# The second FFN of a two-layer backbone: up projection by Strassen's seven products, inner rows kept in DRAM, down projection by resident weight groups

## The chip, the cores and the metric

One core of a Trainium2 chip runs the whole program. The metric is the device time of one execution in microseconds (us), the median of the runs taken. Engines are called by their names in the profile: PE (TensorE matmul), PEld (TensorE weight load), DVE (VectorE), ACT (ScalarE), POOL (GpSimd), SP (SyncE, which here only issues DMAs).

## The reference, cut to what matters

Two layers work on 1152 tokens (1024 latent and 128 context tokens) of width 1024. Each layer has a mixer and then a gated ConvFFN, both between a norm before and a norm and residual after. The change is in the FFN of layer 1, the last work of the program:

```
def conv_ffn(h, w_up, cw, cb, w_down):      # h [1152, 1024], w_up [1024, 5632], w_down [2816, 1024]
    u = dwconv(h @ w_up, cw, 1) + cb        # three taps along the tokens, latent and context apart
    g, val = jnp.split(u, 2, axis=-1)       # 2816 gate and 2816 value channels
    return (jax.nn.gelu(g) * val) @ w_down
```

Everything is float32. The kernel reaches this on PE by splitting each factor x into a high part that the fp32r format holds and a rest, x = xh + xl, and by adding three products: xh yh, xh yl and xl yh (`mm3`, line 80).

## The kernel before, in words

The tokens lie in nine tiles of 128. The inner 2816 channels lie in 22 blocks of 128. The output projection of the mixer (`mixer_out`, L1311) takes the token tiles one after the other: 48 matmuls of 512 columns into two PSUM banks, then `post` (sum of squares on ACT, root on POOL, scaling and residual on DVE) and `pre` (L272: the norm before the FFN, eight transposes on PE, scale and shift on ACT into `h`, the high part on DVE into `hh`, the rest on POOL into `hl`). `hh` and `hl` are whole arrays [128, 8, 1152]: eight slices of the width, all tokens.

`ffn` (L1352) then goes over the 22 blocks. For each it loads the gate's and the value's columns of the up weights (two loads of 512 KB, `wcol`), splits them (ACT the high part `whi`, DVE the rest `wlo`), and for each of three chunks of tokens (386, 386 and 384 columns) and each of the two halves makes 24 matmuls (8 slices of the width, 3 products each; `pps`). The convolution is read straight from PSUM (ACT the middle tap and the bias, DVE the two others into `cc`), then gelu on ACT, the product on DVE, and the split into `mh` (ACT) and `ml` (DVE). After each second block `down` (L1405) adds two blocks' share of the down projection to the sums `acc` of all nine tiles: per tile and half 6 matmuls of 512 columns (`dps`), and a DVE addition. `ffn_end` (L1422) makes the last norm and residual and stores the result.

Buffers come from pools: a tag with n buffers hands them out in turn, and a buffer is filled again when its last reader is done. A pool that is opened over the room of closed ones can be used when those are released. The order of the instructions on each engine is fixed when the program is built, by a planner that takes the program's order as the priority and its own estimate of durations; each engine then works through its queue in that order and waits where an input isn't there.

## Time and profile before

| | |
|---|---|
| runs | 3004.41, 3001.33, 2997.97 us; median 3001.33 |
| profiled execution | span 2997.2 us (the page gives no device time of this execution of its own; the span lies within the runs shown) |
| busy | PE 94%, PEld 85%, DVE 68%, ACT 37%, POOL 27% of the span |
| layer 1's output projection ends, second FFN begins | about 2158 us into the span |
| last matmul begins | 2988.4 us into the span |

PE's busy time is modelled: a matmul of 384 columns is shown as 0.33 us long although the next one starts 0.17 us later. What a matmul costs in a stream is therefore read from the distance between starts.

### The profile page before, as it was taken

The numbers are of one execution on the slowest core, as the hardware profiler recorded it, in microseconds if no ns is written. First come the engines' busy times: TensorE is split into PE (matmuls) and PEld (weight loads), VectorE is DVE, ScalarE is ACT, GpSimd is POOL, SyncE is SP. The second block draws the span as 40 slices with busy tenths as digits, with TensorE's granted clock in tenths as the row PEclk, the third lists the DMA queues.
The fourth block names the chain that finished last, engine by engine and source line by source line (L and its number), as shares of the span: only waits on it lengthen the run. The fifth ranks groups of instructions, "written<-read, shape, count | busy, mean of one in ns | idle before, by whom it ended". The sixth has DMA issues, their size and how long they took to land.

```text
span 2997.2 us, 40584 instructions
## 1 busy us (share of the span) xinstructions
PE 2816.8 (94%) x15196; PEld 2557.3 (85%) x15196; DVE 2035.9 (68%) x3572; ACT 1096.7 (37%) x1921; POOL 813.7 (27%) x982
## 2 busy tenths in 40 slices
PE   7976788888999999999999989999999999999998
PEld 3874566777789999999999979997899999999997
DVE  6777765988668888888655685455455555555557
ACT  5222113766454222322222365554532222222222
POOL 2699972877131000000000151112300000000001
PEclk9998899999999999999999999999999999999999
DMA  6434447552642333323211131124411111111113
GB/s 222 142 86 107 117 138 200 137 116 75 193 146 89 98 99 96 97 91 93 62 43 57 64 122 55 53 88 146 138 46 43 43 43 43 43 43 43 43 36 134
DMA packets 298835, 279.45 MB, mean 93 GB/s; under 512 B 45454, under 2 KB 259682, under 8 KB 298638
## 3 DMA queue, kind: packets, MB, share of 16 engines
q1 hardware_dynamic: 266168, 238.51, 25.8%
q0 software_dynamic: 14912, 23.21, 3.1%
q10 hardware_dynamic: 17558, 15.14, 1.8%
q8 instruction: 119, 1.95, 0.3%
q14 instruction: 78, 0.64, 0.1%
HBM read 220.59 MB, written 56.20 MB: 92 GB/s over the span
## 4 chain that ended last, share of the span: by engine, by line
PE 69%; DVE 6%; ACT 3%; issue 2%; DMA 1%; POOL 1%; ACTq 0%; DVEq 0%; POOLq 0%; SPq 0%
PE pps L87 43%; PE dps L87 16%; PE ops L87 6%; DVE e L1077 1%; DVE nb L1060 1%; PE sA L1055 1%; ACT e L1066 1%; PE gps L87 1%; PE tps L284 1%; DVE wh L1102 0%; DVE s L1114 0%; PE ops L1145 0%; DMA mw<-w_mod 0%; POOL hl L290 0%; PE gps L759 0%
## 5 line engine op out<-in xcount | busy, mean ns | idle before, releaser
L87 PE MATMUL pps<-hh,whi 128*128 128x384 f32 (+1 forms) x2880 | 977.0, 339 | 1.1 <-ACT whi L97 0.7
L87 PE MATMUL pps<-hh,wlo 128*128 128x384 f32 (+1 forms) x2880 | 974.7, 339 | 2.2 <-DVE wlo L99 2.2
L87 PE MATMUL pps<-hl,whi 128*128 128x384 f32 (+1 forms) x2880 | 974.7, 339 | 0.6 <-POOL hl L798 0.4
L87 PEld LDWEIGHTS pps<-hh,whi 128*128 128x128 f32 x2880 | 546.1, 190 | 17.5 <-issue 3.2
L87 PEld LDWEIGHTS pps<-hh,wlo 128*128 128x128 f32 x2880 | 545.6, 189 | 15.2 <-DVE wlo L99 3.2
L87 PEld LDWEIGHTS pps<-hl,whi 128*128 128x128 f32 x2880 | 546.4, 190 | 8.1 <-DVE hl L798 0.7
L99 POOL TENSOR_TENSOR wlo<-wr,whi 128x1024 fp32r<-128x1024 f32 x44 | 109.2, 2487 | 1455.3 <-PE dps L87 1162.5
L1374 DVE SCALAR_TENSOR_TENSOR cc<-pps,cvc,cc 128x255 f32<-128x255 f32 (+1 forms) x704 | 342.0, 511 | 145.0 <-ACT cc L1371 139.8
L1420 DVE TENSOR_TENSOR acc<-acc,dps 128x512 f32<-128x512 f32 x360 | 245.9, 683 | 232.5 <-PE dps L87 231.5
L1371 ACT ACTIVATE cc<-pps,cvc 128x383 f32<-128x383 f32 (+2 forms) x264 | 175.0, 665 | 414.1 <-PE pps L87 393.3
L87 PE MATMUL dps<-whi,mh 128*128 128x512 f32 x792 | 311.8, 394 | 1.2 <-DVE acc L1420 1.2
L87 PE MATMUL dps<-whi,ml 128*128 128x512 f32 x792 | 312.0, 394 | 0.0
L87 PE MATMUL dps<-wlo,mh 128*128 128x512 f32 x792 | 310.5, 392 | 0.0
L97 ACT ACTIVATE whi<-wr 128x1024 fp32r<-128x1024 f32 x168 | 177.7, 1059 | 278.3 <-PE pps L87 196.6
L99 DVE TENSOR_TENSOR wlo<-wr,whi 128x1024 fp32r<-128x1024 f32 x124 | 153.9, 1243 | 85.4 <-PE pps L87 70.4
L231 DVE SCALAR_TENSOR_TENSOR macc<-mw,sil,macc 128x256 f32<-128x256 f32 x392 | 174.9, 482 | 18.9 <-DMA mw<-w_mod 18.1
L87 PEld LDWEIGHTS dps<-whi,ml 128*128 128x128 f32 x792 | 148.8, 188 | 33.7
L87 PEld LDWEIGHTS dps<-whi,mh 128*128 128x128 f32 x792 | 149.2, 188 | 20.8 <-DVE acc L1420 2.4
L87 PEld LDWEIGHTS dps<-wlo,mh 128*128 128x128 f32 x792 | 149.2, 188 | 18.8
L1389 ACT ACTIVATE cc<-cc 128x385 f32<-128x385 f32 x132 | 69.3, 525 | 248.1 <-DVE cc L1374 232.2
L1104 POOL TENSOR_TENSOR wl<-wf,wh 128x512 fp32r<-128x512 f32 (+2 forms) x96 | 144.4, 1523 | 52.5 <-DVE ra L1074 44.1
L1394 DVE TENSOR_TENSOR ml<-cc,mh 128x385 fp32r<-128x385 f32 x132 | 118.2, 899 | 34.2 <-ACT mh L1393 34.2
(356 smaller groups left out, 4171.6 us busy)
## 6 DMA issues: line engine op xcount, KB each, us to landing
wr<-ffn_w_up SPq DMA_DIRECT2D x88, 512.0 KB
mw<-w_mod SPq DMA_DIRECT2D x224, 128.0 KB
x<-x SPq DMA_DIRECT2D x45, 512.0 KB
wr<-ffn_w_down SPq DMA_DIRECT2D x44, 512.0 KB
wm<-w_mod SPq DMA_DIRECT2D x40, 512.0 KB
k<-kh POOLq DMA_DIRECT2D x8, 1408.0 KB, 6.4
wr<-w_in_cd SPq DMA_DIRECT2D x20, 512.0 KB
yr<-y SPq DMA_DIRECT2D x17, 512.0 KB
```

What stands on the lines that cost most here:

```text
L87: nc.tensor.matmul(ps, x, y, start=first and i == 0 and j == 0, stop=last and i == n - 1 and j == 2)
L97: nc.scalar.activation(hi, raw, AF.Copy)
L99: (eng or nc.vector).tensor_tensor(lo, raw, f(hi), op=OP.subtract)
L231: nc.vector.scalar_tensor_tensor(acc[v], wt, s, acc[v], op0=OP.mult, op1=OP.add)
L284: nc.tensor.transpose(ps[:, i], tmp[:, b * 128:(b + 1) * 128], self.id)
L1055: pin(nc.tensor.matmul(A[:, c:c + w], heads[u.h, 2][:, m, u.q0:u.q0 + 128], heads[u.h, m][:, j, u.k0 + c:u.k0 + c + w], start=j == 0, stop ...
L1104: pin((nc.vector if late else nc.gpsimd).tensor_tensor(vl, u.wf[b][:, :k], f(vh), op=OP.subtract))
L1371: nc.scalar.activation(cc[:, :no], ps[:, q:q + no], AF.Identity, bias=cw[3], scale=cw[1])
L1374: nc.vector.scalar_tensor_tensor(cc[:, oa - o0:ob - o0], ps[:, oa + d - i0:ob + d - i0], cw[j], cc[:, oa - o0:ob - o0], op0=OP.mult, op1=O ...
L1389: nc.scalar.activation(cc[:, :no], cc[:, :no], AF.Gelu_apprx_tanh)
L1394: nc.vector.tensor_tensor(ml[:, o0:o1], g[1][:, :no], f(mh[:, o0:o1]), op=OP.subtract)
L1420: nc.vector.tensor_tensor(acc[t][:, sl], acc[t][:, sl], ps, op=OP.add)
```

## The change

Only layer 1's FFN is changed; layer 0's still runs `ffn` and `ffn_end`. Beside that, the pools are opened in another order, one small load of layer 0's output projection (`rb`) takes a buffer of `cv` and no longer one of its own pool, and comments are gone.

The up projection of one block, gate and value together, is a product of a 2 x 2 arrangement of weights (gate or value by first or second half of the width) with a 2 x 2 arrangement of inputs (half of the width by half of the tokens, 576 each). The new code makes it by seven products instead of eight (Strassen's in Winograd's form). Each has 4 slices of the width, 3 split products and two matmuls of 288 columns, 24 matmuls into two PSUM banks (`prod`). Sums of weights are formed on POOL in the weight tiles themselves and then split (`pair`); sums of inputs (`forms`: T1, T2, T3, T4, each in a high part and a rest) are formed once. The results are put together by additions on DVE (with one addend in PSUM) and POOL. `up_rest` then runs the convolution from SBUF over whole rows of 1152 tokens, and writes the high part and the rest of the inner rows to DRAM. `down2` keeps the split down weights of 8, 7 and 7 blocks in SBUF and for each group goes over the nine tiles, with the inner rows read back through POOL's DMA queue; the sums start in the first group (ACT), grow in the others (DVE), and in the third the tile's norm, residual and store follow at once (`ffn_fin`).

All these buffers lie in pools that are opened after the pools of the stage before are closed: `big` (inputs by quarters) on the right side, `big2` (T2, T1, T4), `wru` (raw weights and split pairs, 8 buffers) and `midu` (8 buffers) on the left over the room of the output projection, and four PSUM buffers of two banks each, which are all eight banks. The down stage's pools in turn lie over those of the up stage.

```
+    def pair(self, raw, eng, pool=None):
+        p = (pool or self.wr).tile([128, 2] + shape[1:], F32R, ...)
+        self.nc.scalar.activation(p[:, 0], raw, AF.Copy)
+        eng.tensor_tensor(p[:, 1], raw, f(p[:, 0]), op=OP.subtract)
+    def prod(self, p, y):
+        ps = self.bank2("sps")
+        w = HT // 2
+        steps = [(p[:, x, k], y[j][:, k]) for k in range(4) for x, j in ((0, 0), (0, 1), (1, 0))]
+        for n, (x, y) in enumerate(steps):
+            for c in range(2):
+                nc.tensor.matmul(ps[:, c, :w], x, y[:, c * w:c * w + w], start=n == 0, stop=n == len(steps) - 1)
+    def forms(self, H):
...
+        for k in range(4):
+            A, B, C = (self.mid_tile([128, 2, HT], "tf") for _ in range(3))
+            whole(C[:, 0], 0, 1, k, V)
+            whole(A[:, 0], 0, 0, k, G)
+            whole(A[:, 1], 1, 1, k, V)
+            V.tensor_tensor(A[:, 0], C[:, 0], A[:, 0], op=OP.subtract)
+            V.tensor_tensor(B[:, 0], A[:, 1], A[:, 0], op=OP.subtract)
+            put(T2, k, B[:, 0], V)
+            put(T1, k, A[:, 0], V)
+            whole(B[:, 1], 1, 0, k, G)
+            V.tensor_tensor(A[:, 1], A[:, 1], C[:, 0], op=OP.subtract)
+            put(T3, k, A[:, 1], G)
+            V.tensor_tensor(B[:, 1], B[:, 0], B[:, 1], op=OP.subtract)
+            put(T4, k, B[:, 1], G)
+        def block(fb):                       # in up()
...
+            tt(G, S1, A21, A22, OP.add)
+            tt(G, S2, S1, A11, OP.subtract)
...
+            A.activation(x, P(A11, B11, V), AF.Copy)
+            tt(G, A21, A11, A21, OP.subtract)
+            p = P(A12, B21, G)
+            tt(V, c11, x, p, OP.add)
+            tt(G, A12, A12, S2, OP.subtract)
+            A.activation(q_, P(A12, B22, V), AF.Copy)
+            yield
+            T1, T2, T3, T4 = F
+            p = P(S2, T2, G)
+            tt(V, x, x, p, OP.add)
...
+            A.activation(y, P(S1, T1, V), AF.Copy)
+            tt(G, c12, x, y, OP.add)
+            tt(G, c12, c12, q_, OP.add)
+            p = P(A21, T3, G)
+            tt(V, z, x, p, OP.add)
...
+            p = P(A22, T4, V)
+            tt(G, c22, z, y, OP.add)
+            tt(V, c21, z, p, OP.subtract)
+            self.up_rest(l, fb, C)
+            yield
+        next(bs[0])
+        next(bs[1])
+        F.extend(self.forms(H))
+        for fb in range(NFB):
+            next(bs[fb])
+            if fb > 0 and fb + 1 < NFB:
+                next(bs[fb + 1])
+    def up_rest(self, l, fb, C):             # for s in 0 (gate), 1 (value): ACT middle tap, four DVE taps from SBUF, gelu
...
+        nc.vector.tensor_tensor(m, h, m, op=OP.mult)
+        nc.scalar.activation(h.bitcast(F32R), m, AF.Copy)
+        nc.vector.tensor_tensor(m, m, h, op=OP.subtract)
+        for x, y in enumerate((h, m)):
+            nc.sync.dma_start(self.scratch(f"m{l}", [2, NFB, 128, T])[x, fb], y)
+    def down2(self, l, finish):              # GROUPS = (range(0, 8), range(8, 15), range(15, 22))
...
+        for gi, fbs in enumerate(self.GROUPS):
+            for t in range(NT):
+                mt = self.dm.tile([128, 2, n, 128], F32R, tag="dm", name=self.nm("mt"))
+                for x in range(2):
+                    nc.gpsimd.dma_start(mt[:, x], m[x, fbs[0]:fbs[-1] + 1, :, t * 128:t * 128 + 128].rearrange("f p t -> p f t"))
...
+                            nc.tensor.matmul(ps[:, h], mt[:, x, i], W[fb][:, y, h * 512:h * 512 + 512], ...)
+                if gi == 0:
+                    nc.scalar.activation(acc[t], pv, AF.Copy)
+                else:
+                    nc.vector.tensor_tensor(acc[t], acc[t], pv, op=OP.add)
...
+        self.big2, self.wr, self.mid = P("big2", 6), P("wru", 8), P("midu", 8)
+        self.ps = P("psu", 4, space=PSUM)
+        self.up(1, H)
```

## Rows read from the trace of the kernel before

**Rows 1.** The page: busy us and share of each engine, instructions
```profile
PE 2816.8 (94%) x15196; PEld 2557.3 (85%) x15196; DVE 2035.9 (68%) x3572; ACT 1096.7 (37%) x1921; POOL 813.7 (27%) x982
```

**Rows 2.** Windows (stretch; busy per engine; clock; DMA share; GB/s): the second FFN
```profile
2170.70:2988.90 818.20, 818.07 (x4296) 767.12 (x4293) 467.07 (x739) 226.96 (x350) 62.59 (x40) 1.00 0.16 50
```

**Rows 3.** The chain of waits, in order of time: one period of the FFN
```profile
2311.03 2.76 PE dps L87 x12
...
2386.43 2.76 PE dps L87 x12
```

**Rows 4.** PE's timeline (start, us, operation): distance of starts at 384 and 512 columns
```profile
2201.86 0.34 PE L87 MATMUL pps<-hh,whi 128*128 128x384 f32 x1
...
2210.02 0.33 PE L87 MATMUL pps<-hh,wlo 128*128 128x384 f32 x1
...
2984.07 0.39 PE L87 MATMUL dps<-wlo,mh 128*128 128x512 f32 x1
...
2988.38 0.39 PE L87 MATMUL dps<-whi,ml 128*128 128x512 f32 x1
```

**Rows 5.** PE's timeline in the S5 gate: a stream of 24 at 288 columns
```profile
744.21 3.31 PE L759 MATMUL gps<-gg,gw 128*128 128x288 f32 x24
747.36 0.50 PE L1109 MATMUL ops<-ones,o 128*128 128x1 f32 x4
```

**Rows 6.** Timeline where the output projection ends and the FFN begins
```profile
2157.89 1.03 PE L284 MATMUL tps<-misc,tmp 128*128 128x128 f32 x8
2159.98 1.28 DVE L270 SCALAR_TENSOR_TENSOR x<-tmp,rs,x 128x1024 f32<-128x1024 f32 x1 [0.35 <-POOL rs L144]
2167.41 0.75 DVE L277 TENSOR_SCALAR tmp<-x,q 128x1024 f32<-128x1024 f32 x1 [2.10 <-POOL q L144]
2170.58 2.91 ACT L287 ACTIVATE h<-tps,mc,mc 128x128 f32<-128x128 f32 x8 [1.86 <-PE tps L284]
```

**Rows 7.** Timeline where attention's PSUM pools replace those of the projections
```profile
498.25 0.49 ACT L940 ACTIVATE qr<-pps 128x384 f32<-128x384 f32 x1 [3.67 <-PE pps L87]
498.84 2.56 PE L1055 MATMUL sA<-k,q 128*128 128x512 f32 x12 [0.63 <-issue]
```

**Rows 8.** Timelines of POOL and DVE: the same operations alone and side by side
```profile
2172.63 1.29 POOL L290 TENSOR_TENSOR hl<-h,hh 128x512 fp32r<-128x512 f32 x1 [5.26 <-DVE hh L289]
...
2161.68 2.21 POOL L290 TENSOR_TENSOR hl<-h,hh 128x512 fp32r<-128x512 f32 x1 [1.74 <-DVE hh L289]
2161.52 1.22 DVE L99 TENSOR_TENSOR wlo<-wr,whi 128x1024 fp32r<-128x1024 f32 x1
...
2938.22 2.42 POOL L99 TENSOR_TENSOR wlo<-wr,whi 128x1024 fp32r<-128x1024 f32 x1 [13.74 <-PE dps L87]
2938.25 0.69 DVE L1420 TENSOR_TENSOR acc<-acc,dps 128x512 f32<-128x512 f32 x1 [1.33 <-PE dps L87]
2938.85 2.20 DVE L1394 TENSOR_TENSOR ml<-cc,mh 128x385 fp32r<-128x385 f32 x1
```

**Rows 9.** Groups by line and form (busy us, mean ns): DVE's and ACT's prices
```profile
L954 DVE TENSOR_TENSOR qr<-qr,qsw 128x1152 f32<-128x1152 f32 x8 | 11.0, 1379 | 3.9 <-ACT qsw L953 3.9
L1392 DVE TENSOR_TENSOR cc<-cc,cc 128x385 f32<-128x385 f32 x44 | 24.5, 556 | 0.5
L1485 DVE SCALAR_TENSOR_TENSOR t<-t,lruc,t 128x1023 f32<-128x1023 f32 x8 | 10.2, 1280 | 3.3 <-ACT t L1501 3.3
L953 ACT ACTIVATE qsw<-qr 128x1152 fp32r<-128x1152 f32 x8 | 9.3, 1165 | 34.1 <-DVE qr L952 34.1
```

**Rows 10.** DMA issues (KB each, us to landing): the whole run, then 470 to 520
```profile
y<-t POOLq DMA_DIRECT2D x2, 576.0 KB, 3.2
...
v<-vh POOLq DMA_DIRECT2D x1, 1408.0 KB, 14.8
```

**Rows 11.** Window between the layers, where PE pauses (columns as rows 2)
```profile
1750.00:1760.00 10.00, 3.56 (x17) 2.31 (x16) 8.63 (x11) 7.75 (x20) 9.29 (x12) 0.84 0.51 180
```

**Rows 12.** DVE's timeline at the end: the last addition of the down projection
```profile
2989.48 0.68 DVE L1420 TENSOR_TENSOR acc<-acc,dps 128x512 f32<-128x512 f32 x1
```

More of the change, by code (lines that the diff above doesn't have):

```diff
@@ L277, in pre @@
         nc.vector.tensor_scalar(tmp, x, rs, None, op0=OP.mult)
-        ts = slice(t * 128, t * 128 + 128)
         for q in range(2):
@@ new lines, in pair, with bank2 @@
+    def pair(self, raw, eng, pool=None):
+        shape = list(raw.shape)
+        p = (pool or self.wr).tile([128, 2] + shape[1:], F32R, tag="wd" if pool else "wr", name=self.nm("wp"))
+        self.nc.scalar.activation(p[:, 0], raw, AF.Copy)
+        eng.tensor_tensor(p[:, 1], raw, f(p[:, 0]), op=OP.subtract)
+        return p
+    def bank2(self, name):
+        return self.ps.tile([128, 2, 512], F32, tag="ps", name=self.nm(name))
+    def prod(self, p, y):
+        nc = self.nc
+        ps = self.bank2("sps")
[4 more added lines that the diff above has]
+                nc.tensor.matmul(ps[:, c, :w], x, y[:, c * w:c * w + w], start=n == 0, stop=n == len(steps) - 1)
+        return ps[:, :, :w]
@@ new lines, in forms, with whole, put @@
+    def forms(self, H):
+        nc = self.nc
+        V, G = nc.vector, nc.gpsimd
+        T2, T1, T4 = ([self.big2.tile([128, 4, HT], F32R, tag="big2", name=self.nm(n + s)) for s in "hl"] for n in ("T2", "T1", "T4"))
+        T3 = H.b[0, 1]
+        def whole(out, q, n, k, eng):
+            h, l = H.b[q, n]
+            eng.tensor_tensor(out, f(h[:, k]), f(l[:, k]), op=OP.add)
+        def put(t, k, src, eng):
+            nc.scalar.activation(t[0][:, k], src, AF.Copy)
+            eng.tensor_tensor(t[1][:, k], src, f(t[0][:, k]), op=OP.subtract)
+        for k in range(4):
[12 more added lines that the diff above has]
+            put(T4, k, B[:, 1], G)
+        return T1, T2, T3, T4
@@ new lines, with weight @@
+    GROUPS = (range(0, 8), range(8, 15), range(15, 22))
+    def down2(self, l, finish):
+        nc = self.nc
+        w_down = self.a["ffn_w_down"][l]
+        m = self.scratch(f"m{l}", [2, NFB, 128, T])
+        W, acc = {}, []
+        def weight(fb):
+            raw = self.wr_tile([128, D], "wd")
+            nc.sync.dma_start(raw, w_down[fb * 128:fb * 128 + 128])
+            W[fb] = self.pair(raw, nc.gpsimd if fb % 2 else nc.vector, self.wd)
+        for fb in self.GROUPS[0]:
+            weight(fb)
+        todo = list(range(8, NFB))
+        for gi, fbs in enumerate(self.GROUPS):
+            n = len(fbs)
+            for t in range(NT):
+                mt = self.dm.tile([128, 2, n, 128], F32R, tag="dm", name=self.nm("mt"))
+                for x in range(2):
+                    nc.gpsimd.dma_start(mt[:, x], m[x, fbs[0]:fbs[-1] + 1, :, t * 128:t * 128 + 128].rearrange("f p t -> p f t"))
+                ps = self.bank2("dps")
+                for i, fb in enumerate(fbs):
+                    for j, (x, y) in enumerate(((0, 0), (1, 0), (0, 1))):
+                        for h in range(2):
+                            nc.tensor.matmul(ps[:, h], mt[:, x, i], W[fb][:, y, h * 512:h * 512 + 512],
+                                             start=i == 0 and j == 0, stop=i == n - 1 and j == 2)
+                pv = ps.rearrange("p h c -> p (h c)")
+                if gi == 0:
+                    acc.append(self.acc.tile([128, D], F32, tag="acc", name=self.nm("acc")))
+                    nc.scalar.activation(acc[t], pv, AF.Copy)
+                else:
+                    nc.vector.tensor_tensor(acc[t], acc[t], pv, op=OP.add)
+                if todo and todo[0] < self.GROUPS[min(gi + 1, 2)][-1] + 1:
+                    weight(todo.pop(0))
+                if gi == 2:
+                    finish(t, acc[t], pv)
@@ new lines, in ffn_fin @@
+    def ffn_fin(self, t, y, junk, xin, ga, out):
+        nc = self.nc
+        x = self.wr_tile([128, D], "x")
+        nc.sync.dma_start(x, xin)
+        rs = self.rstd(self.sumsq([y], junk), D)
+        for i in range(2):
+            sl = slice(i * 512, i * 512 + 512)
+            nc.vector.scalar_tensor_tensor(y[:, sl], y[:, sl], rs, ga[:, sl], op0=OP.mult, op1=OP.mult)
+            nc.vector.tensor_tensor(y[:, sl], y[:, sl], x[:, sl], op=OP.add)
+            nc.sync.dma_start(out[:, sl], y[:, sl])
```

140 lines of the change are left out of this document (103 added, 37 removed).

## The prediction

> **What bounds the kernel now.** I read the page first: PE is busy 94% of the span and the next engine, DVE, 68% [rows 1]. A share over the whole span says little of one stage, so I asked for the window of the second FFN: PE is busy 818.07 of 818.20 us at full clock (1.00), DVE 467, ACT 227, POOL 63, and the DMA engines 0.16 of the time [rows 2]. So in this stage nothing but the number and the pitch of the matmuls counts. The chain agrees: it is PE alone, with a period of 75.40 us (2311.03 to 2386.43) for two blocks of the up projection and one call of `down` [rows 3].
>
> The price of a matmul is the distance of starts, since the shown lengths overlap. 48 matmuls of 384 columns, first and last start in [rows 4]: 8.16 us over 47 steps, 173.6 ns. 20 of 512 columns: 4.31 us over 19 steps, 226.8 ns. At 2.4 GHz the columns alone are 160.0 and 213.3 ns, so each matmul carries 13.5 ns more, whatever its length.
>
> **The change part by part.**
>
> *Up projection, saved.* The down part of a period is 108 matmuls, 24.5 us; what is left of 75.40 us is 50.9 us for two blocks, 25.45 us for one, 560.0 us for 22 [rows 3, 4]. The new block has 7 products of 24 matmuls of 288 columns, 3,696 in all. By 120 + 13.5 ns one takes 133.5 ns; the S5 gate runs this size already, 24 of them from 744.21 until the next group at 747.36: 131.3 ns [rows 5]. I take 133: 3.19 us a product, 22.3 us a block, 491.6 us in all. **Saved: 68.4 us** (66.5 to 74.7). The smaller matmuls give back a part of the eighth that the method saves: 288 columns bear the same 13.5 ns as 384.
>
> *Down projection.* 1,188 matmuls of 512 columns before and after, 269.4 us: nothing, as long as weights and inner rows arrive in time. Each tile of a group of 8 needs 1 MB of inner rows through POOL's queue in 10.9 us. The nearest transfer (v<-vh, also short pieces on POOL's queue) took 14.8 us for 1408 KB in a busy stretch [rows 10], 10.8 us for 1 MB: just enough, with three buffers ahead. I count 1 us.
>
> *First pause, where the up stage begins.* Now the last tile's chain (post, norm, transposes, scale and shift) lies beside the FFN's first chunks, and PE runs on. It runs from 2157.9, where the last output matmul is followed by the transposes of the tile before, over 2167.41 (DVE's scaling) to 2173.49, the end of ACT's reading of its own transposes [rows 6]. The new PSUM pool takes all eight banks, so its first product can't start before that last reading. Such a change of pools is in the trace: attention's first matmul starts at 498.84, 0.10 us after ACT's last reading of the projections' PSUM ended, though other banks had long been free [rows 7]. Without the FFN's own ACT work and without PE's queue of chunks (2.4 us lie between DVE's result and ACT's first reading) the chain is some 4 us shorter: I put the first product at 2169.7. **Cost: 12 us, of which 10 idle** (6 to 14). A pause also costs clock: in the window where PE was busy 3.56 of 10 us the granted clock is 0.84 [rows 11]; after a longer pause I count 2 us for running at 1.2 GHz, inside the 12 here.
>
> *Second pause, T1 to T4.* Six products (two blocks' first halves) need no T: PE has work to about 2190.6. For each of 4 slices DVE has 8 additions of 576 columns and POOL 4. Here lies what the trace shows of POOL and DVE side by side [rows 8]: POOL's subtraction of 512 columns takes 1.29 us alone and 2.21 beside a DVE operation with two SBUF inputs; DVE's of 385 columns, 0.556 alone [rows 9], takes 2.20 and ends 0.41 us after the POOL operation it met. Each waits for the other, whole instructions long. DVE's addition with one input in PSUM (0.69) isn't held [rows 8]. What the one that waits saves is its fixed 0.15 us. From 385 and 1152 columns (0.556, 1.379 [rows 9]) 576 columns are 0.76 us on DVE; POOL by proportion 1.45. Less 0.15 each, a slice is 8 x 0.61 + 4 x 1.30 = 10.1 us. POOL also owes 10 operations on the first two blocks' weights (11.4 us), DVE 4 (2.2). From 2170 the last slice of T2 is there after 13.6 + 3 x 10.1 + 3 = 47 us less what POOL did before: about 2215. PE would have ended the first product with a T at 2193.8. **Cost: 21 us** (8, if only POOL's own 26.7 us count and half is hidden; 28 at most).
>
> *Steady state, the shared port.* PE needs 22.3 us a block. ACT has about 12 us: it is no bound. POOL: 7 operations of 512 and 3 of 576 columns, 7 x 1.29 + 3 x 1.45 = 13.4 us. DVE with two SBUF inputs: 4 remainders of 512 (0.69 each), 4 long taps (1.28 [rows 9]), 4 short ones (some 0.3), 2 of 1152 (1.38), together 11.8 us; the taps are new in this list, since they now read SBUF and not PSUM. Neither engine is full, but as they exclude one another the sum counts: 25.2 us by whole durations, 21.6 if each of the 24 hides its 0.15 us behind the other. PE's 22.3 lies between. Weight buffers let the pairs run 3 to 4 products ahead and four PSUM buffers take 9 us of late evacuation, so I let PE stay the bound with 0.2 us lost a block: **cost 4 us** (0 to 60).
>
> The Trainium skill, GPSIMD Engine Reference, § 8 Key points, says that POOL shares its SBUF interfaces with VectorE and that they contend when a DVE instruction has two SBUF inputs. This trace agrees (2.21 against 1.29 us), and the rule speaks against this change; whoever adds the engines up apart from each other would have 13.4 and 14.9 us and no cost here.
>
> *Third pause, up to down.* The split down weights fill 120 KB of each partition and so lie over the up stage's work buffers, whose last reader is the store of the last block's inner rows. Behind the last product: DVE's addition (0.8), ACT's middle tap (some 1.2, as L953 [rows 9]), four taps (3.2), the product (1.38), ACT's high part (1.17), DVE's remainder (1.38), the store (3.2, as y<-t [rows 10]), with hand-overs 13 us. Then the first weight of 1024 columns is split: ACT some 1.05 (1.165 for 1152 [rows 9]), DVE 1.22 [rows 8], and PE starts 15.5 us after the last product. The next seven weights follow at ACT's, DVE's and POOL's (2.42 [rows 8]) pace, and the raw ones come through four buffers; PE fills with the first three tiles meanwhile and loses some 3 us more, and 2 for the clock. **Cost: 20 us** (13 to 28).
>
> *The rest.* The last tile's tail now begins with an addition of 1024 columns and has four half operations in a row; before, 7.7 us pass from the last addition's start to the end of the span [rows 12]. I add 1.4. POOL's and SP's queues: per block SP issues two loads and two stores, a store waits for the remainder, and the loads of a later block stand behind it; they are some 10 us ahead, which covers it while DVE isn't late. Layer 0's other pools: 0 (3 either way).
>
> **Sum**, against the profiled execution's span of 2997.2: -68.4 + 1 + 12 + 21 + 4 + 20 + 1.4 = -9.0, so 2988.2. Its device time isn't shown; the median 3001.33 lies 4.1 above its span, and with the same 4.1 I predict **2992 us**.
>
> **The rivals.**
>
> *The port binds (slower).* If the shared port sets the block at 24.3 us, between 21.6 and 25.2, the 21 blocks after the start lose 2.0 us each, 42 in place of 4: 3030. It decides as soon as a block's two sums, with the time in which both engines wait for something else, exceed 22.3 us: 0.7 us of such waiting is enough. For it: the sum is within 4% of PE's need, and the planner fixed the queues. Against: the long lead of pairs and PSUM.
>
> *The pauses are covered (faster).* If buffers come free one by one and the planner brings other work forward, the pauses cost 6, 8 and 13 us, 26 less: 2966. Against it stands the hand-over at 498.84.
>
> *The down stage waits for its reads (slower).* At 12 us a tile in place of 10.9 in the first group and 10.5 in place of 9.5 in the others, the 27 tiles cost 27 us: 3018. For it the 14.8 us; against it the weights, which come a group ahead, and a DMA share that was 0.16.
>
> *A shorter pitch.* The Trainium skill, TensorE: Matmul & The Clock Gate, § Back-to-back issue gap, gives the isolated gap as the columns at 2.4 GHz and 2.5 ns more; at 288 columns an estimate by that page is 122.5 ns. The trace has 131.3 and 133.5 and, at 512, 226.8, so I give it little. As a mechanism: if the second matmul on the same weights saved its 13.5 ns, half of 3,696 would save 25 us: 2967. Attention's first twelve, by the code 8 of 512 and 4 of 256 columns in runs on the same weights, take 2.56 us [rows 7]; less the last one's length of some 0.28 that is 2.28, and 8 x 226.8 + 3 x 120 ns are 2.17: no such gain shows.
>
> *The change doesn't do what it says:* the seven products are all there and PE had no idle time to hide the eighth; I leave it no chance of weight.
>
> **How the numbers follow.** PE stays the bound with three pauses, 0.42 (2980 to 3006); the port binds, 0.34 (3010 to 3050); covered pauses 0.13; reads 0.08; pitch 0.03. About 0.2%, 6 us, is what a measurement can tell from no change (2995.3 to 3007.3). Of the first case 0.31 lies below, 0.11 inside; of the second 0.31 above, 0.03 inside. Faster 0.31 + 0.13 + 0.03 = 0.47; same 0.14; slower 0.31 + 0.08 = 0.39. Range for 8 in 10: 2965 to 3036.
>
> **What would show it.** Right: PE busy over 97% in a window of the steady up stage and starts 22.3 to 22.6 us apart for a block; one gap of some 7 and 3 us round 2165, one near 2195 to 2215 that waits for the DVE and POOL additions of `forms`, one of some 15 us between the last product and the first `dps`. Wrong: a block of 24 us with PE waiting for pairs or PSUM while POOL's and DVE's operations are longer than alone (the port); gaps under 8 us (covered pauses); PE waiting for `mt` in each tile (reads).

## The result: 149 us slower, two thirds of it ahead of the changed stage

The changed kernel takes 3149.15 us (median of 4 runs, 3147.86 to 3149.71), the kernel before on the same chip 2999.72: ratio 1.0492, 95% interval 1.0477 to 1.0507. The forecast was 2992 us, with a range of 2965 to 3036. The profiled execution has a span of 3147.8 us.

The page says less than one would like: PE is busy for as long as before [rows 1], with 528 instructions more, so the 150 us are time in which PE stands. (A matmul at the lower clock counts as busy for longer, so this share hides a part of the loss.)

```profile
PE 2822.0 (90%) x15724; PEld 2536.6 (81%) x15724; DVE 2057.8 (65%) x3321; ACT 1156.5 (37%) x1946; POOL 1250.4 (40%) x1263
```

The next view is a table by stretch, and not only of the stage that was changed. In windows of 100 us before and after first differ by much at 800 us, in layer 0's output projection. The window of the kernel before, then of the changed one (columns as rows 2):

```profile
800.00:900.00 100.00, 98.88 (x475) 83.09 (x474) 60.05 (x79) 54.66 (x128) 34.93 (x49) 1.00 0.44 148
```

```profile
800.00:900.00 100.00, 60.89 (x231) 48.14 (x230) 29.03 (x36) 25.69 (x60) 18.70 (x24) 0.76 0.23 74
```

Tile after tile starts 24 to 26 us apart there, 11.8 before; the projection takes 208.8 us from its first to its last matmul and not 107.5. What PE waits for between 780 and 1010 us (total, times, longest):

```profile
PE tps L317 <- DVE tmp L311: 48.5, 8, 6.1
PE ops L121 <- ACT yh L1367: 28.5, 8, 4.3
```

Eight times each, once per tile, and in turn. The order in the kernel before, then one tile in the timeline of the changed one:

```profile
852.84 0.37 SPq L1321 DMA_DIRECT2D rb<-rs  x1
...
858.78 1.03 PE L284 MATMUL tps<-misc,tmp 128*128 128x128 f32 x8
...
859.57 1.17 PE L87 MATMUL ops<-wo,yh 128*128 128x512 f32 x4
```

```profile
855.10 0.33 SPq L1378 DMA_DIRECT2D x<-x  x1
855.48 0.43 SPq L1353 DMA_DIRECT2D rb<-rs  x1
...
858.00 1.97 PE L317 MATMUL tps<-misc,tmp 128*128 128x128 f32 x8 [6.07 <-DVE tmp L311]
...
860.75 0.43 DVE L322 CAST hh<-h 128x512 fp32r<-128x512 f32 x1 [2.81 <-ACT h L320]
861.21 1.85 DVE L1365 SCALAR_TENSOR_TENSOR yr<-yr,dag,rb 128x512 f32<-128x512 f32 x1
...
864.26 2.07 PE L121 MATMUL ops<-wo,yh 128*128 128x512 f32 x4 [4.29 <-ACT yh L1367]
```

SP issues the load of `rb` for the next tile only behind the store of this tile's `x`, so the next tile's scaling, split and matmuls come behind this tile's post norm. DVE's queue holds the cast of this tile's `h` ahead of the next tile's scaling, and PE's queue holds this tile's transposes ahead of the next tile's 48 matmuls. In the kernel before the load at 852.84 is that of two tiles further on, and the transposes at 858.78 are of the tile before the one whose 48 matmuls have just been issued. In the changed kernel the chain of a tile no longer lies beside the matmuls of another. The clock of 0.76 is a mean: these pauses let it fall to 1.2 GHz for part of each tile (the eight matmuls of a transpose take 1.97 us here, 1.03 before [rows 6]).

The second FFN itself begins 109 us late and takes 880 us in place of 839 (2157.89 [rows 6] to the end of the span). Its stretches: last output matmul to first product, the products without a T (all but the end of the sixth), the T forms, on to the steady state, the steady state, the pause, the down stage (behind it lies a tail of 8.6 us):

```profile
2267.30:2286.00 18.70, 2.80 (x17) 2.22 (x15) 7.57 (x10) 9.08 (x23) 11.80 (x12) 0.58 0.46 141
2286.00:2304.50 18.50, 18.50 (x122) 18.50 (x123) 3.41 (x6) 5.47 (x10) 9.79 (x9) 0.87 0.00 1
2304.50:2345.30 40.80, 25.25 (x96) 19.91 (x94) 40.45 (x33) 12.21 (x19) 30.46 (x17) 0.63 0.00 0
2345.30:2380.00 34.70, 29.63 (x190) 28.85 (x191) 28.74 (x26) 15.92 (x20) 25.39 (x15) 0.85 0.14 39
2380.00:2837.00 457.00, 442.70 (x3286) 438.22 (x3285) 343.36 (x354) 205.46 (x270) 336.87 (x191) 1.00 0.28 98
2837.00:2858.40 21.40, 1.10 (x9) 0.90 (x7) 9.53 (x12) 6.25 (x6) 8.13 (x8) 0.58 1.19 303
2858.40:3139.20 280.80, 280.12 (x1188) 225.05 (x1188) 65.86 (x61) 39.86 (x46) 80.75 (x75) 0.99 0.63 151
```

The third line shows the T stage: DVE busy for 40.45 of 40.80 us with 33 operations, 1.23 us each, where an addition of 576 columns alone takes 0.74. In the steady state the chain is PE with a hole, here of 0.87 us in a period of 23.51 us (blocks take 22.4 to 24.0, 23.4 in the mean); the addition at its end frees a PSUM buffer:

```profile
2566.67 22.64 PE sps L1497 x168
2589.31 0.74 DVE C L1536
2590.05 0.14 issue
2590.18 1.83 PE sps L1497 x12
```

Here operations of one kind and size show two lengths (groups between 2420 and 2820 us: busy, mean ns):

```profile
L1483 DVE TENSOR_TENSOR wp<-wg,wp 128x512 fp32r<-128x512 f32 x34 | 51.4, 1513 | 59.5 <-ACT wp L1482 59.5
L1536 POOL TENSOR_TENSOR C<-Y 128x576 f32<-128x576 f32 x17 | 40.9, 2406 | 0.0
L1536 POOL TENSOR_TENSOR ws<-wv 128x512 f32<-128x512 f32 x17 | 40.3, 2373 | 94.7 <-DMA wv<-ffn_w_up 94.7
L1536 POOL TENSOR_TENSOR wg<-wg,ws 128x512 f32<-128x512 f32 x17 | 21.9, 1287 | 1.3
L1483 DVE TENSOR_TENSOR wp<-ws,wp 128x512 fp32r<-128x512 f32 x18 | 12.5, 692 | 10.0 <-ACT wp L1482 10.0
```

DVE's remainders of 512 columns take 0.692 us or 1.513 in the mean, POOL's sums of 512 columns 1.287 or 2.373, which fits the two lengths in [rows 8], alone and side by side.

### The profile page after: what moved, and what is told of

Its sections match the earlier page's. It is cut to its first block, busy times and chain, and to the rows that moved or that the text cites. A ratio compares the mean times of both kernels' runs of the same rounds, so it can differ in the third digit from the quotient of the medians.

```text
span 3147.8 us, 42033 instructions
## 1 busy us (share of the span) xinstructions
PE 2822.0 (90%) x15724; PEld 2536.6 (81%) x15724; DVE 2057.8 (65%) x3321; ACT 1156.5 (37%) x1946; POOL 1250.4 (40%) x1263
## 4 chain that ended last, share of the span: by engine, by line
PE 51%; DVE 6%; POOL 5%; issue 3%; DMA 2%; ACT 2%; ACTq 0%; POOLq 0%; DVEq 0%; SPq 0%
PE pps L121 23%; PE dps L1635 8%; PE sps L1497 8%; PE dps L121 7%; PE ops L121 3%; DVE cc L1598 1%; POOL C L1536 1%; POOL ws L1536 1%; DMA wv<-ffn_w_up 1%; PE gps L121 1%; POOL wv L1536 1%; DMA mw<-w_mod 1%; ACT cc L1594 1%; POOL wp L1483 0%; DVE C L1536 0%
## 5 line engine op out<-in xcount | busy, mean ns | idle before, releaser
L121 PE MATMUL pps<-hh,whi 128*128 128x384 f32 (+1 forms) x1824 | 625.3, 343 | 1.0 <-ACT whi L131 0.5
L121 PE MATMUL pps<-hh,wlo 128*128 128x384 f32 (+1 forms) x1824 | 623.5, 342 | 2.2 <-DVE wlo L133 2.2
L121 PE MATMUL pps<-hl,whi 128*128 128x384 f32 (+1 forms) x1824 | 623.7, 342 | 0.4 <-POOL hl L831 0.4
L121 PEld LDWEIGHTS pps<-hh,whi 128*128 128x128 f32 x1824 | 349.6, 192 | 11.9 <-issue 3.2
L121 PEld LDWEIGHTS pps<-hh,wlo 128*128 128x128 f32 x1824 | 349.3, 192 | 8.4 <-DVE wlo L133 3.2
L121 PEld LDWEIGHTS pps<-hl,whi 128*128 128x128 f32 x1824 | 349.7, 192 | 4.5 <-POOL hl L831 0.7
L1635 PE MATMUL dps<-wp,mt 128*128 128x512 f32 x1188 | 280.2, 398 | 20.3 <-ACT wp L1482 20.3
L1635 PEld LDWEIGHTS dps<-wp,mt 128*128 128x128 f32 x1188 | 225.2, 190 | 75.1 <-issue 20.5
L1497 PE MATMUL sps<-hh,wp 128*128 128x288 f32 x1408 | 257.5, 300 | 10.5 <-DVE wp L1483 2.5
L1497 PEld LDWEIGHTS sps<-hh,wp 128*128 128x128 f32 x1408 | 213.9, 192 | 12.8 <-issue 4.8
L265 DVE SCALAR_TENSOR_TENSOR macc<-mw,sil,macc 128x256 f32<-128x256 f32 x392 | 175.6, 482 | 22.3 <-DMA mw<-w_mod 22.0
```

What stands on the lines that cost most here:

```text
L121: nc.tensor.matmul(ps, x, y, start=first and i == 0 and j == 0, stop=last and i == n - 1 and j == 2)
L265: nc.vector.scalar_tensor_tensor(acc[v], wt, s, acc[v], op0=OP.mult, op1=OP.add)
L1497: nc.tensor.matmul(ps[:, c, :w], x, y[:, c * w:c * w + w], start=n == 0, stop=n == len(steps) - 1)
L1635: nc.tensor.matmul(ps[:, h], mt[:, x, i], W[fb][:, y, h * 512:h * 512 + 512], start=i == 0 and j == 0, stop=i == n - 1 and j == 2)
```

## The experiments

Times with a ratio are medians of several runs beside the kernel before, those without are of one execution. The time of a block is the distance of the starts of its first matmul and the next block's.

### One small buffer (e1, e2)

The kernel before with `rb` moved, and the changed kernel with `rb` moved back:

```
e1, in the kernel before:
-                rb = self.rsb.tile([128, 4, 128], F32, tag="rb", ...)
+                rb = self.cv.tile([128, 4, 128], F32, tag="cv", ...)
e2, in the changed kernel: the same line the other way, and
+            with self.P("rsb", 1, side="right") as self.rsb:
                 self.mixer_out(0, W, self.xsrc, x1, Whole(hh, hl))
```

> The kernel before with one edit: layer 0's small load rb takes a buffer of cv (4 buffers) in place of its own pool; the old second FFN stays. Theory R: of the 149 us lost, some 109 lie here. In the changed kernel layer 0's output projection has a period of 25 us per token tile in place of 11.8, since rb's load now waits for a cv buffer, stands in SP's queue behind the store of the tile before, and PE's queue has the transposes of each tile ahead of the next tile's projection. Then this kernel takes 2999.7 + 109 = 3109 us (3100 to 3115), and PE is busy about 61% of the stretch 800 to 1000. Rival O: the other order of the pools (mid, A and B opened elsewhere) is the cause; then this kernel takes 2997 to 3003 us and the tile period stays 11.8 us.

> The changed kernel with one edit: rb has a pool of its own again, the rest as changed. Theory R: 3149 - 109 = 3040 us (3034 to 3048), tile period of layer 0's output projection 11.8 us, the second FFN as before this edit (880 us from the end of the output projection to the end of the span). Rival O: still 3145 to 3150 us.

e1: 3103.21 us, ratio 1.0337 (1.0318 to 1.0356), 103 us more than before with the old FFN in place. e2: 3047.67 us, ratio 1.0157 (1.0140 to 1.0174), 101 us less than the changed kernel. The window 800 to 900 of e1, then of e2:

```profile
800.00:900.00 100.00, 59.72 (x228) 47.02 (x226) 30.58 (x42) 26.88 (x64) 22.23 (x26) 0.80 0.23 74
```

```profile
800.00:900.00 100.00, 99.63 (x469) 82.48 (x468) 54.21 (x72) 49.14 (x116) 31.59 (x46) 1.00 0.41 136
```

So the buffer is the main cause: 103 of 149 us; 41 are the FFN's, and some 5 are left. Most of these lie ahead of layer 0's output projection: from attention's first matmul to that projection's first, 287.5 us pass before and 288.3 in e1, but 291.3 in the changed kernel, 294.2 in e2 and 292.2 to 298.2 in its other variants. So 4 to 11 us go with the other order of the pools, which all of them have; no run takes it alone. A load of 256 KB that no row of before shows as a cost weighed more than the whole loss in the FFN. With `cv`'s four buffers shared by `rb` and two `h` of each tile, the planner laid out SP's, DVE's and PE's queues in another order. By the code, the old order could not have stayed without a pause: a tile takes three of the four buffers, so `rb` gets the buffer of the second `h` of the tile two before its own, and in the kernel before that `h` came only behind the matmuls of the tile between, while `rb` was loaded ahead of them. No run tests this, and why the planner chose this order is not shown.

### The steady block: buffers, order, load (w10, g1, g3, g2)

```
w10 = e2 with  self.wr = P("wru", 10)                    # 8 before
g1  = e2 with forms and pool as in c1 below, forms behind the first block's first half, and
+            self.up_rest(l, fb, C, tt(V, c21, z, p, OP.subtract))
+                    if s == 0: self.behind(i, c21)      # each tap of the gate behind c21 on DVE
g3  = g1 with 10 buffers and the forms on both engines
g2  = g1 without c21's edit, and
-            tt(G, S1, A21, A22, OP.add)                 # and S2, A11 - A21, A12 - S2
+            tt(V, S1, A21, A22, OP.add)
```

> As e2_after_rb_own_pool, with 10 buffers for weights and pairs in place of 8. In the steady up stage of the changed kernel a block takes 23.5 us though its 168 matmuls need 22.4. Theory ring: the load of the values' weights waits for a buffer, POOL's sums wait for the load (5.4 us per block), ACT's and DVE's convolution wait for POOL's c12, and DVE frees the buffer behind the taps; the ring has 23.5 us. With two more buffers the load comes earlier and the block falls to 22.4 to 22.6 us, some 18 us less over the stage: 3022 us. Rival port: the operations of POOL and DVE that exclude one another fill the block by themselves; then more buffers change nothing, 23.4 to 23.5 us a block, 3040 us.

w10: 3091.8 us, 44 more than e2; blocks of 24.3 to 31.7 us, 26 on average. More buffers made it worse, which neither theory had foretold. The waits between 2400 and 2740 us show that the load was hardly late any more (19.5 us in all; in e2 POOL waited 67.1 us for it between 2400 and 2680), and what was:

```profile
POOL wp L1483 <- ACT wp L1482: 116.9, 38, 5.6
PE sps L1497 <- DVE C L1536: 32.9, 15, 3.5
POOL ws L1536 <- DMA wv<-ffn_w_up: 19.5, 13, 2.9
```

POOL's queue now held the next pairs' remainders, which wait for ACT's high parts, ahead of c12, so that ACT's and DVE's convolution came later. That this order is the whole cause is argued from the waits, not tested.

> As e2_after_rb_own_pool, with the split pool of c1 and the forms on DVE, and two edits of order. (1) forms is written ahead of the second block's first half. In e2 the forms' first additions stand in DVE's queue behind the addition of the second block's second product, which waits for PE, so DVE idles 16 us and begins them 10 us after their inputs are there. Theory order: from the first product to the start of the fourth block, 106 us in e2 and 96 us in c1, falls to 85 to 90 us. Rival port: all the forms' time is work of DVE, begun earlier it only holds up the pairs: 94 to 98 us as in c1. (2) Up stage: the addition c21, which frees the last product's PSUM buffer, is put in DVE's queue ahead of the gate's taps. In e2 and c1 PE waits 1 us a block at the T2 product; the buffer it needs is held 9.8 us after the product's end, because c21 stands behind two taps that wait for ACT and, before that, for POOL's c12. Theory queue: the wait goes, 22.4 to 22.6 us a block in place of 23.5. Rival port: DVE and POOL fill the block whatever their order, 23.5 us as before. By both theories 3032 - 8 - 18 = 3006 us, by both rivals 3030.

> As w10_ten_weight_buffers (10 buffers, forms on both engines, 25.7 us a block on average), with the split pool, forms ahead of the second block's first half, and c21 ahead of the gate's taps. Theory queue: what made w10 slow is that DVE's queue was built in another order, with more pairs between c21 and its product; with c21 ahead a block takes 22.4 to 22.6 us. Rival: the time of a block is set by something else (POOL's operations waiting for DVE's); 24 us or more remain. The forms on both engines: if the order was the cause of the late T forms, the stretch from the first product to the start of the fourth block is at most 95 us here, too; if the port was, 100 us or more.

g1: 3031.05 us, 23.5 us a block as before: the theory of DVE's queue fell. The order of the forms won 4 us (first product to fourth block 91.8 us, 95.7 in c1), between the two theories. g3: 3073.39 us, blocks of 22.4 to 27.9 us: with 10 buffers, too, c21's place was not the cause. Its stretch from the first product to the fourth block takes 106.3 us, as in e2 (106.1): with the forms on both engines the earlier place in the queue won nothing (w10, with 10 buffers and the old place, has 99.8), as the rival had it.

> As g1_c21_first, without its edit (2); in its place the four sums of weights (S1, S2 and the two that follow) go from POOL to DVE. POOL's 512-column sums took 1.29 to 2.37 us, DVE's addition of this size 0.55 to 0.69. Theory port: what counts is the sum of POOL's and DVE's exclusive operations; it falls by 4 x (1.25 - 0.6) = 2.6 us and the block to 22.4 to 22.6 us. Theory queue: c21 still stands behind the gate's taps, but POOL reaches c12 earlier, so its wait shrinks or goes, too. Rival: DVE is the engine that is late, and 2.5 us more on it make a block 24 to 26 us.

g2: 3000.67 us, and 22.4 us a block from the sixth on, without a hole. In the window 2400 to 2680 of e2, then of g2:

```profile
2400.00:2680.00 280.00, 269.36 (x2003) 266.93 (x2002) 203.28 (x214) 127.59 (x168) 211.50 (x120) 1.00 0.28 96
```

```profile
2400.00:2680.00 280.00, 280.00 (x2105) 280.00 (x2104) 241.30 (x277) 136.54 (x178) 128.90 (x77) 1.00 0.29 101
```

Neither POOL (76%) nor DVE (73%) was full in e2; 82.6 us of POOL's time went away for 38.0 us on DVE, and the loss in the steady block with it.

### What lengthens a block when DVE gets more (d1, d2, d3)

```
d1 = g2 with, behind S2 in each block:   for _ in range(4): V.tensor_tensor(dum, A21, A22, op=OP.add)
d2 = g2 with, in the same place:         for _ in range(5): V.tensor_copy(dum, A21)
d3 = g2 with  self.wr = P("wru", 10)
```

> As g2_sums_on_dve (22.4 us a block, PE without a pause), with 4 operations added to each block on DVE: additions of 512 columns with two inputs in SBUF, 0.6 to 0.69 us each, whose result nobody reads. Theory port (POOL's operations and DVE's with two SBUF inputs exclude one another, and their sum counts): the sum, which moving the weight sums had lowered by 2.6 us, is back where it was in e2, and so is the block: 23.3 to 23.8 us, total 3020 us. Rival path (what helped was that POOL comes to c12 earlier, not the sum): POOL's work is as in g2, DVE has 19.3 + 2.6 = 21.9 us, under 22.4: the block stays at 22.4 to 22.6 us, 3001 us.

> As d1_added_two_input_ops, but the added operations are 5 copies of 512 columns, with one input, 0.42 to 0.43 us each: 2.1 us more on DVE. Theory port: a copy doesn't exclude POOL, the block stays at 22.4 to 22.6 us, 3001 us. Rival DVE: any work on DVE costs alike, so this block is as long as that of d1, less 0.5 us.

> As g2_sums_on_dve, with 10 buffers for weights and pairs. w10 and g3 with 10 buffers needed 25.7 us a block, more than with 8; in w10 POOL waited 117 us in 340 for ACT's high parts, since with more buffers the next block's pairs stand ahead of c12 in its queue. Theory: what 10 buffers add is that longer way to c12, which counts only as POOL and DVE are full; with the sums on DVE the block stays near 22.4 us, at most 23. Rival: the order of the queues costs by itself: 24 us or more here, too.

d1: 3051.59 us, 24.8 us a block on average, more than either theory had; d2: 3045.23 us, 24.1 us; d3: 2998.84 us, 22.4 us. d1 refutes the theory that only POOL's way to c12 counts. But d2 refutes mine that a copy is free: it was nearly as dear, as its rival foretold. The window 2400 to 2680 of d1, and window and group of the copies of d2:

```profile
2400.00:2680.00 280.00, 261.96 (x1915) 259.74 (x1915) 273.88 (x296) 118.69 (x160) 140.03 (x69) 0.98 0.27 93
```

```profile
2400.00:2680.00 280.00, 262.52 (x1952) 260.07 (x1950) 271.74 (x311) 121.12 (x163) 129.57 (x72) 1.00 0.27 95
L1547 DVE COPY dum<-wv 128x512 f32<-128x512 f32 x58 | 42.6, 735 | 0.4
```

In both DVE is all but full (98 and 97% of the time): its own work and the time for which POOL holds it add up to more than PE's 22.4 us. A copy that takes 0.41 us alone takes 0.735 in the mean, so it is held, too. The Trainium skill, SBUF — State Buffer, § Who interferes with whom, says it: copies can enter a mode that takes the interface that DVE shares with POOL, so not only operations with two SBUF inputs contend; this trace agrees (735 against 410 ns). d3 shows that 10 buffers do no harm once POOL is relieved. What d1 and d2 don't separate for e2, where DVE was not full, is how much of its 1.1 us a block came from the held operations' length and how much from POOL's being a step on the way from the load to c12; both went with the same edit.

### The T forms and the pause between the stages (c1, h1, h4, h5)

```
c1 = e2 with
-            whole(A[:, 0], 0, 0, k, G)                  # and B21, the remainders of T3 and T4
+            whole(A[:, 0], 0, 0, k, V)
     down2: for h in range(2): outside the loops over blocks and products
-                self.wr, self.wd = P("wrd", 4, side="right"), P("wd", 15, side="right")
+                self.wr, self.wd, self.wd2 = P("wrd", 4, ...), P("wd", 7, ...), P("wd2", 8, ...)
h1 = g2, forms ahead of the first block, and
-        self.ps = P("psu", 4, space=PSUM)
+        self.ps = P("psu", 2, space=PSUM); and P("psv", 1), P("psw", 1), taken in turn
h4 = h1, three first halves ahead of the T products, 9 buffers in midu
h5 = g2 with the PSUM pool of h1
```

> As e2_after_rb_own_pool, with three edits in three stretches that don't overlap, each read from its own stretch. (1) forms: its POOL additions and remainders go to DVE. While they run, DVE's operations take 1.23 us in the mean where they take 0.68 to 0.75 alone. Theory port: alone on the port, 12 operations of 0.7 us are 8.4 us for a slice in place of 10.4, and the stretch with T1 to T4 gets 6 to 10 us shorter. Rival: the two engines work side by side, so 16 more operations on DVE make it 8 to 12 us longer. (2) down: the two halves of a tile one after the other, not in turn. The 512-column matmuls of the down stage start 233.3 ns apart, those of the kernel before 226.8. If taking two PSUM banks in turn is the cause, 227 ns and 7.7 us less over 1188; if the stationary inner rows are, 233 ns as now. (3) the pool of the down weights is cut in two, so that the first 7 lie over the inputs alone and not over the buffer that the last store reads. The pause between the stages is 21 us; if the pool as a whole makes the first weight wait for that store, it falls to 8 to 13 us; if something else holds the first product, it stays at 20 to 22.

c1: 3033.77 us. (1) From the first product to the fourth block 95.7 us in place of 106.1: with 16 more operations DVE had the forms done in 35.7 us in place of 45.3, as the port theory said. (2) 233.3 ns between the down stage's matmuls as before: taking the banks in turn is not the cause. (3) PE's pause fell from 19.7 to 9.1 us, since a pool opened over several old ones waits for the last of them. What is late next (timeline of c1) is the read of inner rows, behind c22 in POOL's queue; the weights' splits are late, too, and the down stage itself takes 284.1 us, 4.9 more than in e2:

```profile
2738.72 0.77 PE L1635 MATMUL dps<-wp,mt 128*128 128x512 f32 x1 [8.90 <-DMA mt<-m]
```

> As g2_sums_on_dve, with two edits at the start of the up stage. (1) forms is written ahead of the first block, so that its additions no longer stand in DVE's queue behind the addition of the first block's second product (in g2 DVE idles from 2187.3 to 2190.2 and the forms begin at 2192.9, though the last inputs are there at 2186.7). Theory order: the forms begin and end 5 to 6 us earlier, and so does the first block with a T. (2) the PSUM pool of the up stage is cut in three (two buffers, one, one), so that the first products wait for the banks under them and not for the last reading of the transposes. Theory pool: the first product starts 2 to 6 us earlier; as the forms decide when PE goes on, that alone is worth nothing. Together 3000.7 - 6 = 2995 us (2991 to 2998). Rival: the forms now hold up the pairs of the first products on DVE, PE starts later, and nothing is gained: 2998 to 3004 us.

> As h1_forms_ahead_psum_split, with the first halves of three blocks, not two, ahead of the T products, and 9 work buffers in place of 8. In g2 PE has 19 us of products without a T and stands for 18 us in all until the forms are done; a third block's first half is 9.6 us of work for that time. Theory: 6 to 9 us less than h1, 2986 to 2990 us. Rival buffers: the third block's three weight tiles take buffers from the pairs (8 in all), the loads come later, and a steady block takes 23 us or more: 3000 us or more. Rival order: DVE and ACT must make three more pairs while the forms run, the forms end as much later as PE has work more: as h1.

> As g2_sums_on_dve, with the PSUM pool of the up stage cut in three and forms where g2 has it, behind the first block's first half. h1, with forms ahead of that too, began its first product 13 us earlier than g2 and won 2 us: ACT's copy of a product, which frees its PSUM buffer, stood behind the forms' copies in ACT's queue, and PE waited 27.8 us once. Theory queue: with the copy and the addition of the first block ahead of the forms that wait goes; the forms begin at 2188 as in h1, 5 us earlier than in g2: 2995 us (2992 to 2998). Rival: the forms' 33 us of DVE work behind the last tile's chain set the end, and they end as in g2: 2999 to 3002 us.

h1: 3001.31 us, ratio 1.0003 (0.9994 to 1.0012). The cut pool did start the first product earlier (5.6 us after the last output matmul, 15.9 in g2), and the forms began at 2187.97, but PE then waited once for 27.8 us (waits, 2150 to 3130):

```profile
PE sps L1500 <- ACT X L1554: 27.8, 1, 27.8
```

ACT's copy that frees the buffer stood behind the forms' copies. h4: 3010.52 us, ratio 1.0032 (1.0019 to 1.0044). PE waited 26.2 us for the same copy, the first product with a T began 17.7 us later than in h1 (2242.0 and 2224.3), and the fourth to seventh block took 25.0, 22.8, 23.4 and 22.4 us. The total is the one that the rival of buffers had (3000 us or more), but its steady block of 23 us did not come: later blocks take 22.4. h5: 3000.08 us, ratio 0.9994 (0.9985 to 1.0003): counted from the last output matmul, its fourth block starts 2 us earlier than g2's. In g2, h1 and h5 the forms' 48 operations on DVE take 37 to 41 us and end 59 to 66 us after the last output matmul; h1's end first, and PE's wait takes that back. None of the three orders gained more than these 2 us.

### The forms on the engine that stands (h6, h7)

```
+        def sum_pe(t, k, *terms):                       # I: unit matrix, with sign + and -
+            steps = [(I[:, n, :128], x[:, k]) for n, b in terms for x in H.b[b]]
+            ... matmuls of 288 columns into one PSUM buffer
+            nc.scalar.activation(two(t[0][:, k]), ps, AF.Copy)
+            V.tensor_tensor(two(t[1][:, k]), ps, f(two(t[0][:, k])), op=OP.subtract)
h6 = h5 with sum_pe for slices 2 and 3, h7 for all four
```

> As h5_psum_split_only, with two of the four slices of the forms made by PE, which stands idle meanwhile: the sums of high parts and remainders as matmuls with a unit matrix of either sign, 22 of them (44 matmuls of 288 columns, 5.9 us) a slice; ACT takes the high part and DVE the remainder from PSUM. DVE's work on the forms falls from 48 to 32 operations (35 to 24 us), and 8 of these have one input in PSUM. Theory: the forms end 9 to 11 us earlier than in h5, of which PE's 11.7 us of added work take a part in time in which it was idle anyway: 2984 to 2990 us. Rival: the sums take the PSUM buffers of the products and wait for ACT and DVE to read them, so that PE stands as long as before: 2995 us or more.

> As h6_forms_half_on_pe, with all four slices on PE: 176 matmuls of 288 columns, 23.5 us, and only 16 remainders left on DVE (12 us). Theory: PE becomes the bound of this stretch, without a pause, and the up stage begins its steady state some 5 us later than with h6: 2988 to 2995 us. Rival: DVE, freed of 24 us, lets the pairs and the sums of weights go ahead, and it is as fast as h6 or faster by some us.

h6: 2992.9 us, ratio 0.9972 (0.9960 to 0.9983): 0.3% faster than the kernel before, clear of noise, and between the theory's 2984 to 2990 and the rival's 2995. Counted from the last output matmul, its fourth block starts 8.6 us earlier than g2's. The stretch from first product to steady state, and the steady state:

```profile
2172.20:2225.00 52.80, 46.49 (x300) 44.77 (x301) 38.23 (x54) 23.73 (x44) 14.78 (x12) 0.87 0.12 35
2225.00:2690.00 465.00, 465.00 (x3493) 465.00 (x3493) 397.45 (x455) 223.24 (x287) 212.26 (x126) 1.00 0.29 100
```

h7: 2998.91 us, ratio 0.9991 (0.9982 to 1.0000). Counted in the same way, its fourth block starts 6.3 us later than h6's: all 176 sum matmuls are too many for PE, none leaves DVE too much.

From the last output matmul to the end of the span, the second FFN takes 839.5 us before, 881.0 in the changed kernel, 878.7 in e2, 830.8 in g2 and 821.6 in h6. So by these profiled executions the new FFN is in the end 18 us faster than the old one; of these 9 are lost again before it begins, most of them ahead of layer 0's output projection, as said at e2, and h6 as a whole is 8 us faster.

## Why the prediction was wrong, step by step

**"Layer 0's other pools: 0 (3 either way)" is the step that failed.** The small load's borrowed buffer measured 103 us (e1) and 101 us (e2), and the other order of the pools goes with another 4 to 11. I had read the one-line edit as a matter of room, and costed it without a row. A buffer from a tag that others use is a wait: it names who must be done before the load can start, and here the new wait came with another order in SP's, DVE's and PE's queues. The rows that would have warned were at hand: before, PE is busy for 98.88 of 100 us in this stretch, and the load at 852.84 is issued two tiles ahead.

**First pause, 12 us:** 18.7 (PE's slow clock behind it, some 2 us, is counted in the second). The chain is the one that I described, but its root is late: POOL did the root `q` behind three operations on the new stage's first weights, and another ahead of `qv`.

```profile
2275.35 0.19 POOL L175 TENSOR_SCALAR qv<-ssq 128x1 f32<-128x1 f32 x1
2275.62 1.26 POOL L1483 TENSOR_TENSOR wp<-wg,wp 128x512 fp32r<-128x512 f32 x1
2276.84 1.26 POOL L1536 TENSOR_TENSOR ws<-ws,wg 128x512 f32<-128x512 f32 x1
2278.06 1.26 POOL L1536 TENSOR_TENSOR wv<-wg,wv 128x512 f32<-128x512 f32 x1
2279.28 0.55 POOL L178 TENSOR_TENSOR q<-qv,mhalf 128x1 f32<-128x1 f32 x1
```

With these sums on DVE the pause falls by 3.2 us of the 7 (from the start of the last output matmul to the first product 19.1 us in g1, 15.9 in g2).

That the PSUM pool as a whole held the first product was right: cut in three, and nothing else changed, it let PE start 5.6 us after the last output matmul in place of 15.9 (h5 against g2).

**Second pause, 21 us:** about 40. From 2286 to 2380 us lie 408 matmuls, 54 us at 133 ns, in 94: some 2 are lost ahead of the T stage, 28 in it and 9 behind it. The mechanism (POOL and DVE hold one another up) was right, and the size was not. The last slice of T2 came 61 us after the first product where 47 had been worked out. The forms began 19 us after it, not 13.6: their first addition stood in DVE's queue behind the addition of the second block's second product and began at 2305.1, 16 us after POOL had written the last of the inputs. Then three slices and T2's part of the fourth took 42 us, not 33. What the runs show to count is the hold-up of the two engines more than the queue: all forms on DVE won 10.4 us (c1), the queue's order 4 more (g1), and the order with the forms on both engines nothing (g3, which has 10 buffers too).

**Steady state, 4 us:** about 20, 3286 matmuls in 457 us (437 at 133 ns). I put the port's sum at 21.6 to 25.2 us and let PE's 22.3 win; 23.5 came out, between. The rival "the port binds" had the place and the sign. My term "0.2 us lost a block" rested on leads of pairs and PSUM that did not help here; by the traces POOL's c12, ACT's middle tap and DVE's taps make one chain through them. What of the 1.1 us a block is this chain and what the held operations is not shown.

**Third pause, 20 us:** 20.5 from the last product to the first matmul of the down stage, where 15.5 had been worked out, and some 3 for the clock in place of the 5 for filling and clock. The reader was the right one (chain of waits): the store of the last inner rows held the weights' pool. It took 6.4 us, not 3.2.

```profile
2850.62 6.40 DMA m<-cc
...
2857.17 1.06 ACT wp L1482
...
2858.32 11.86 PE dps L1635 x38
```

**Down projection, 1 us:** 280.8 us for what I had put at 269.4 and 1, of which some 3 are the slow clock after the pause, counted there. Reads were not late: PE waits for no `mt` in this stage. The pitch is 233.3 ns. I had taken the 226.8 of the last tiles before [rows 4]; twelve matmuls of the period in [rows 3] take 2.76 us, 230 each, so the 13.5 ns that each matmul carries are not the same at every place. The remaining 3 ns, 4 us in all, are not explained; c1 only rules out the order of the banks.

**Saved, 68.4 us:** 63.4, under the 66.5 at the low end. The new block is as forecast: 168 matmuls take 22.4 us in g2, 133.3 ns each. But with the pitch of 230 ns for the down part the old up projection is 25.28 us a block, not 25.45.

Together the FFN came out 50 us above its forecast of 830 us, and the buffer 103: without the buffer the time would have been e2's, 12 us outside the range. So the FFN's own terms, the second pause and the steady block above all, missed the range too. The chance of 0.39 for slower was fair for these risks; what was missing is a rival in which an edit that is not the change's subject decides.

## What to carry to other kernels

Cost every line of a diff by the wait that it adds, the small ones first: a buffer borrowed from a busy tag can cost more than the stage that the change is about. When an added stage runs on two engines that hold one another up, try moving work to the engine whose operation is shorter before changing buffers or order (g2 against w10, g1 and g3), as long as that engine has room (d1, d2), and look for an engine that stands anyway (h6). A pool opened over several old ones starts when the last is free; cut along the old pools' borders, it starts piece by piece.

## What was not expected of the hardware

POOL can be held for far longer than one of DVE's operations lasts. In g2 a subtraction of 512 columns (1.29 us alone) took 11.06 us, while DVE had fifteen operations with two SBUF inputs in a row; it ended 1.2 us after DVE had begun an addition with one input in PSUM, and the operation that DVE began meanwhile took 1.17 us in place of 0.74. In h1 the same subtraction took 19.08 us (from 2202.95) and again ended 1.2 us after DVE had begun such an addition (2220.80). The rows of g2:

```profile
2219.13 0.74 DVE L1513 TENSOR_TENSOR T4l<-tf,T4h 128x576 fp32r<-128x576 f32 x1
2219.32 11.06 POOL L1483 TENSOR_TENSOR wp<-wv,wp 128x512 fp32r<-128x512 f32 x1 [8.62 <-ACT wp L1482]
...
2229.16 0.73 DVE L1536 TENSOR_TENSOR C<-X,sps 128x576 f32<-128x576 f32 x1
2229.82 1.17 DVE L1524 TENSOR_TENSOR tf<-tf,tf 128x576 f32<-128x576 f32 x1
```

The reverse is seen in c1, where a remainder of 1024 columns on DVE (1.22 us alone, [rows 8]) took 7.74 us while POOL issued reads and then made two remainders. A tap with two SBUF inputs beside the same issues took its usual 1.28 us ([rows 9]); why the remainder did not end before POOL's remainders began is open:

```profile
2731.53 5.42 POOL L1630 DMA_DIRECT2D mt<-m  x6
...
2733.77 1.28 DVE L1598 SCALAR_TENSOR_TENSOR cc<-C,cvc,cc 128x1023 f32<-128x1023 f32 x1
2734.97 7.74 DVE L1483 TENSOR_TENSOR wp<-wd,wp 128x1024 fp32r<-128x1024 f32 x1
...
2736.95 4.67 POOL L1483 TENSOR_TENSOR wp<-wd,wp 128x1024 fp32r<-128x1024 f32 x2
```
